# Weight halves of the pair products interleaved word by word in their ring tiles

## The chip, the cores and the metric

The kernel runs on one core of a Trainium2 chip. The metric is the device time of one execution in microseconds (us); lower is better. Five engines work at the same time, each through its own queue in order: TensorE (PE; its weight loads are shown apart as PEld), VectorE (DVE), ScalarE (ACT), GpSimd (POOL) and SyncE (SP), which issues nearly all transfers.

## The reference: what is computed

Two requests of 512 tokens of width 1024 go through the same two layers, each of which adds the output of a mixer to its input:

```python
for i in range(DEPTH):                       # 2
    h = rms_norm(x, norm_g[i], NORM_EPS)
    if i % 2 == 0:
        x = x + diff_attention(h, ...)       # proj = h @ w_in -> q, k, v, gate; o @ w_out
    else:
        x = x + bidir_retention(h, ...)      # proj = h @ w_in -> q, k, v, gate; o @ w_out
return rms_norm(x, final_norm_g, NORM_EPS)
...
proj = h @ w_in                              # (512, 1024) @ (1024, 8192) in layer 0, 6144 columns in layer 1
q, k, v, gate = jnp.split(proj, [...], axis=-1)
```

All in float32. The change concerns the big input projections `h @ w_in` of both layers, for the columns that become q, k and gate.

## The kernel before

**Numbers in two halves.** A float32 operand is split in two: the upper half is the value as a copy into the type fp32r leaves it, the lower half is the rest (value minus upper half, again as fp32r). A product takes three matmuls (`PASSES`: upper x upper, upper x lower, lower x upper), summed in PSUM. The helper `hi_of` (line 399) writes the upper half by a copy on ScalarE (it shows as L400 CAST), `lo_of` (line 402) the lower one by a subtraction on VectorE that reads the upper half back (L403).

**Projection units.** The projections are cut into units (class `Unit`, line 518), each for 256 columns of one weight matrix at two column groups or blocks, computed for both requests. A unit is not done with eight block products but with seven (`SEQ`: P1, P2, P5, P6, P3, P7, P4), each of sums and differences of weight blocks with sums and differences of activation blocks, and the outputs are put together from the seven results. The activation side (`Bop`, made by `make_b`) is split once and lies in SBUF tiles of [128, 2, 512], upper half first, in the tiles named arena and b. The weight side is loaded in raw tiles, combined on VectorE (`combine`, L558, into st tiles) and split into ws tiles, a ring of `WS_BUFS = 7` places of 1024 words per partition.

There are two kinds of units:

- **pair** units (q, k and gate: 24 in the first layer, 16 in the second). The weights are the *stationary* operand: for each of four k-blocks a 128x128 piece of the ws tile is loaded into TensorE, and 512 columns of the activation side stream past. One product is 4 x 3 = 12 matmuls 128x512, each with its own weight load (`pair`, line 596; L599). Both halves of a 128-column block fit in one ws tile: `[P, 2, 4, n]` with n = 128, the upper half in the first 512 words, the lower half in the other 512.
- **wide** units (v). Here the activation side is stationary and the ws tile streams past 256 columns at a time (`wide`, line 603; L609). Each half takes a ws tile of its own.

For the rotary units (q and k) the raw columns are taken in another order: `half_view` (line 944) in the first layer takes runs of 64 columns, `parity_view` (line 947) in the second takes the even and then the odd columns, so that the engines read raw with a step of two words.

**Order.** `projections` (line 778) prepares the splits ahead of the products as far as the seven ws places allow. Every operation is entered in a `Plan` with an estimated cost for its engine; `Plan.arrange` (line 138) plays the engines through by these costs and writes out the order for each queue. The engines then run in that order and wait for each other by semaphores. The attention of the first layer (L1116, L1134, L1181) and the retention of the second (L1315 to L1367) come after the projections of their layer, with the output projections (L891) worked in between.

Of the kernel before, what the change touches and what calls it, by code (L numbers as in the profile page):

```python
# [15 lines left out]
P = 128  # L16
# [237 lines left out]
def trunk_kernel(  # L254
# [42 lines left out]
    def work(tag, shape, bufs, dt=F32, name=None):  # L297
        size = SIZE.get(tag, shape[1])
        return Buf(plan, tag, bufs, lambda i: view(wk, tag, i, size, shape, dt))
# [27 lines left out]
    def ws_t(shape):  # L327
        return work("ws", shape, WS_BUFS, F32R)
# [4 lines left out]
    def st_t(shape, name="st"):  # L333
        return work("st", shape, 3, name=name)
# [36 lines left out]
    def dve(n, fn, r, w, wait=0.0):  # L371
        plan.op("DVE", 0.07 + 0.00104 * n, fn, r, w, wait=wait)
# [26 lines left out]
    def hi_of(n, dst, src, r, w):  # L399
        act(n, lambda: nc.scalar.copy(dst(), src()), r, w)  # L400

    def lo_of(n, dst, src, hi, r, w):
        dve(n, lambda: nc.vector.tensor_tensor(dst(), src(), hi().bitcast(F32), op=ALU.subtract), r, w)  # L403
# [114 lines left out]
    class Unit:  # L518
# [32 lines left out]
        def prep(self, op):  # L551
            x = self.take
            n = 256 if self.wide else P

            def combine(a, b, fn):
                t = st_t([P, 4, n])
                out = ((lambda: self.like(t.t)), t)
                dve(4 * n, lambda: nc.vector.tensor_tensor(out[0](), a[0](), b[0](), op=fn), [a[1], b[1]], [t])  # L558
                return out
            if op == "P1":  # L560
                src = x(0, 0)
            elif op == "P2":
                src = x(0, 1)
            elif op == "P4":
                src = x(1, 1)
            elif op == "P5":
                src = self.s[1] = combine(x(1, 0), x(1, 1), ALU.add)
            elif op == "P6":
                src = self.s[2] = combine(self.s[1], x(0, 0), ALU.subtract)
            elif op == "P3":  # L570
                src = combine(x(0, 1), self.s[2], ALU.subtract)
            else:
                src = combine(x(0, 0), x(1, 0), ALU.subtract)
            if self.wide:
                a, b = ws_t([P, 4, n]), ws_t([P, 4, n])
                hi, lo = ((lambda: a.t), a), ((lambda: b.t), b)
            else:
                s = ws_t([P, 2, 4, n])
                hi, lo = ((lambda: s[:, 0]), (s, 0)), ((lambda: s[:, 1]), (s, 1))
            hi_of(4 * n, lambda: self.like(hi[0]()), src[0], [src[1]], [hi[1]])  # L580
            lo_of(4 * n, lambda: self.like(lo[0]()), src[0], lambda: self.like(hi[0]()), [src[1], hi[1]], [lo[1]])
            self.ops[op] = (hi, lo)
            if op == "P2" and self.early is not None:
                self.early, self.x = None, {}
# [949 lines left out]
```

## Time and profile before

| | |
|---|---|
| median of 3 runs | 1809.73 us (1808.83 to 1810.48) |
| span of the profiled execution, first to last instruction | 1807.0 us |
| median of the runs less that span | 2.7 us |
| granted TensorE clock, mean | 0.999 |
| TensorE busy | 1794.9 us (99%), 10299 matmuls |
| weight loads (PEld) busy | 1558.1 us (86%) |
| VectorE busy | 1477.1 us (82%) |
| ScalarE busy | 895.1 us (50%) |
| GpSimd busy | 169.5 us (9%) |

The profile lists the span of the profiled execution; that execution's time with what lies ahead of the first and behind the last instruction isn't listed apart, so the median of the runs stands in for it. In rows of groups the columns are: line, engine, operation, output<-inputs by the program's tile names, shapes, count, then busy time in us and mean ns of one, then idle time of the engine ahead of the group and what ended it. Busy time counts overlapping instructions once; the mean ns of one is its full length, overlap included. A line can be a helper's, so L400 and L403 stand for all splits of the kernel, told apart by their tiles.

### The profile page before, as it was taken

Reading aid. Unit: us, or ns where it says so; the run is one execution under the profiler, and the core shown is the slowest. Engines: PE = TensorE matmul, PEld = TensorE weight load, DVE = VectorE, ACT = ScalarE, POOL = GpSimd, SP = SyncE. Lnnn points to the kernel's source line nnn. Section 1 sums busy time; section 2 is a strip of 40 time slices with the busy share of each in tenths; the row PEclk is TensorE's granted clock in tenths of the full one; section 3 lists DMA queues with packets and bytes.
Section 4 is the critical chain, followed back from the end, with each engine's and each line's share of the span. In section 5 each row is a group of like instructions: output and inputs, shape, how many; then the busy total and the mean of one; then the engine's idle time right before and its main releaser. Section 6 shows DMA issues by size and latency. Waiting matters only on the chain.

```text
span 1807.0 us, 27780 instructions
## 1 busy us (share of the span) xinstructions
PE 1794.9 (99%) x10299; PEld 1558.1 (86%) x10299; DVE 1477.1 (82%) x2319; ACT 895.1 (50%) x1856; POOL 169.5 (9%) x323
## 2 busy tenths in 40 slices
PE   9999999999999999999999999999999999999998
PEld 6789889898988888888888888898989898888887
DVE  7958787778699888888888897787887967888887
ACT  7753444433434565554555866444434355444346
POOL 1000000000000022222322300000000000111113
PEclk9999999999999999999999999999999999999999
DMA  6444455555545685444554524464657559765662
GB/s 217 134 126 137 161 140 178 184 168 155 174 126 175 201 334 198 178 156 159 190 204 140 190 73 146 140 210 146 205 156 228 151 170 396 272 238 182 225 218 94
DMA packets 162767, 328.81 MB, mean 182 GB/s; under 512 B 12724, under 2 KB 76872, under 8 KB 162632
## 3 DMA queue, kind: packets, MB, share of 16 engines
q1 hardware_dynamic: 162304, 326.71, 54.1%
q8 instruction: 81, 1.33, 0.3%
q14 instruction: 54, 0.44, 0.1%
q10 hardware_dynamic: 328, 0.34, 0.1%
HBM read 209.55 MB, written 117.44 MB: 181 GB/s over the span
## 4 chain that ended last, share of the span: by engine, by line
PE 93%; DVE 2%; DMA 2%; ACT 2%; issue 1%; POOL 0%; SPq 0%; POOLq 0%; DVEq 0%; ACTq 0%
PE pj L599 20%; PE pj L891 19%; PE sc L599 10%; PE pj L609 10%; PE o L599 8%; PE o L1181 5%; PE sc L1116 5%; PE sc L609 5%; PE o L609 2%; PE o L1359 2%; PE tp L1161 2%; PE sc L1315 1%; PE o L1367 1%; PE tp L1339 1%; DMA raw<-in_ret_w_out_dram 1%
## 5 line engine op out<-in xcount | busy, mean ns | idle before, releaser
L891 PE MATMUL pj<-ws,arena 128*128 128x512 f32 x1542 | 391.2, 397 | 0.0
L891 PEld LDWEIGHTS pj<-ws,arena 128*128 128x128 f32 x1542 | 277.7, 188 | 52.7
L599 PE MATMUL pj<-b,ws 128*128 128x512 f32 x1080 | 265.0, 392 | 0.0
L599 PEld LDWEIGHTS pj<-b,ws 128*128 128x128 f32 x1080 | 201.4, 188 | 43.0
L403 DVE TENSOR_TENSOR ws<-st,ws 128x512 fp32r<-128x512 f32 (+1 forms) x192 | 147.9, 774 | 74.8 <-ACT ws L400 56.7
L896 DVE SCALAR_TENSOR_TENSOR b<-pj,crr,b 128x512 f32<-128x512 f32 (+1 forms) x257 | 189.9, 744 | 21.4 <-PE pj L891 21.0
L403 DVE TENSOR_TENSOR ws<-raw,ws 128x512 fp32r<-128x512 f32 (+1 forms) x164 | 141.5, 868 | 71.3 <-ACT ws L400 61.0
L400 ACT CAST ws<-st 128x512 fp32r<-128x512 f32 (+1 forms) x192 | 132.4, 693 | 121.4 <-PE pj L599 36.4
L599 PE MATMUL sc<-arena,ws 128*128 128x512 f32 x768 | 186.8, 392 | 0.0
L599 PE MATMUL o<-arena,ws 128*128 128x512 f32 x744 | 180.0, 393 | 1.1 <-ACT m L385 0.6
L599 PEld LDWEIGHTS sc<-arena,ws 128*128 128x128 f32 x768 | 144.0, 188 | 31.3
L400 ACT CAST ws<-raw 128x512 fp32r<-128x512 f32 (+1 forms) x164 | 125.7, 772 | 87.0 <-PE o L599 45.0
L599 PEld LDWEIGHTS o<-arena,ws 128*128 128x128 f32 x744 | 138.4, 188 | 31.7 <-DVE arena L463 1.4
L599 PE MATMUL pj<-arena,ws 128*128 128x512 f32 x648 | 160.3, 392 | 0.4 <-DVE arena L463 0.4
L599 PEld LDWEIGHTS pj<-arena,ws 128*128 128x128 f32 x648 | 120.8, 188 | 26.7 <-DVE arena L463 0.7
L1134 ACT ACTIVATE b<-sc,nm 128x512 f32<-128x512 f32 x128 | 88.0, 689 | 66.9 <-DVE nm L1124 66.5
L636 ACT COPY c<-pj 128x512 f32<-128x512 f32 x104 | 60.9, 586 | 119.7 <-PE pj L599 66.4
L609 PE MATMUL pj<-ws,b 128*128 128x256 f32 x960 | 116.8, 276 | 0.0
L609 PEld LDWEIGHTS pj<-ws,b 128*128 128x128 f32 x960 | 113.2, 188 | 0.7
L1116 PE MATMUL sc<-arena 128*128 128x512 f32 x384 | 101.2, 395 | 0.3 <-ACT b L1134 0.3
L1181 PEld LDWEIGHTS o<-arena 128*128 128x128 f32 x768 | 93.1, 188 | 2.7
L1181 PE MATMUL o<-arena 128*128 128x256 f32 x768 | 93.7, 278 | 0.0
(207 smaller groups left out, 2855.9 us busy)
## 6 DMA issues: line engine op xcount, KB each, us to landing
qk<-os SPq DMA_DIRECT2D x192, 256.0 KB, 3.6
arena<-qk SPq DMA_DIRECT2D x96, 512.0 KB, 5.8
raw<-in_da_w_in_dram SPq DMA_DIRECT2D x64, 512.0 KB, 5.1
v<-os SPq DMA_DIRECT2D x64, 512.0 KB, 4.3
arena<-v SPq DMA_DIRECT2D x64, 512.0 KB, 4.1
raw<-in_ret_w_in_dram SPq DMA_DIRECT2D x48, 512.0 KB, 4.8
os<-g SPq DMA_DIRECT2D x32, 512.0 KB, 7.4
g<-e SPq DMA_DIRECT2D x48, 256.0 KB, 4.6
```

The costliest lines, as they stand in the source:

```text
L400: act(n, lambda: nc.scalar.copy(dst(), src()), r, w)
L403: dve(n, lambda: nc.vector.tensor_tensor(dst(), src(), hi().bitcast(F32), op=ALU.subtract), r, w)
L599: nc.tensor.matmul(ps.t, a[u][0]()[:, k, :], bt[k][:, v, :], start=(opens and k == 0 and i == 0), stop=(k == 3 and i == 2), skip_group_che ...
L609: nc.tensor.matmul(ps[:, (t % 2) * 256:(t % 2) * 256 + 256], bt[k][:, v, t * P:(t + 1) * P], a[u][0]()[:, k, :], start=(opens and t % 2 == ...
L636: act(S, lambda c=c, ps=ps: nc.scalar.copy(c.t, ps.t), [ps], [c])
L891: nc.tensor.matmul(ps[:, here], o[a][:, e, t * P:(t + 1) * P], u[b][:, e, here], start=(m == 0), stop=(m == 5))
L896: axpy(n, lambda half=half, here=here, ps=ps: nc.vector.scalar_tensor_tensor(half, ps[:, here], rr[:, t % 2:t % 2 + 1], half, op0=ALU.mult ...
L1116: nc.tensor.matmul(s.t, q[:, a, t * P:(t + 1) * P], k[:, b, :], start=(n == 0), stop=(n == 2))
L1134: act(840, lambda j=j, s=s, m=m: nc.scalar.activation(p[:, j, :], s.t, AF.Exp, bias=m.t, accum_out=sm[:, 2 * j + n:2 * j + n + 1]), [s, m] ...
L1161: nc.tensor.transpose(tp[:, j * P:(j + 1) * P], p[:, 0, j * P:(j + 1) * P], ident.t)
L1181: nc.tensor.matmul(o[:, e * 256:(e + 1) * 256], v[b][:, j, e * P:(e + 1) * P], aT[a][:, j, :], start=(n == 0), stop=(n % 12 == 11), skip_g ...
L1359: nc.tensor.matmul(o[:, e * 256:(e + 1) * 256], v_[v][:, 2 * c + j, e * P:(e + 1) * P], a_[:, u, j * 256:(j + 1) * 256], start=(e == 0 and ...
```

## The change

The ws tile of a pair unit keeps its size and its place. Its two halves no longer lie one behind the other: upper and lower half of each weight stand next to each other. So the ScalarE copy writes every second word, the VectorE subtraction reads every second word and writes the words between, and each 128x128 weight load of a pair product reads 128 words with a step of two words.

```diff
             else:
-                s = ws_t([P, 2, 4, n])
-                hi, lo = ((lambda: s[:, 0]), (s, 0)), ((lambda: s[:, 1]), (s, 1))
+                s = ws_t([P, 4, n, 2])
+                hi, lo = ((lambda: s[:, :, :, 0]), (s, 0)), ((lambda: s[:, :, :, 1]), (s, 1))
             hi_of(4 * n, lambda: self.like(hi[0]()), src[0], [src[1]], [hi[1]])
             lo_of(4 * n, lambda: self.like(lo[0]()), src[0], lambda: self.like(hi[0]()), [src[1], hi[1]], [lo[1]])
```

## The prediction

> **What bounds the kernel now.** I read the page first, then the groups by line with shapes kept apart, the waits of PE, the chain of waits in order of time, the timeline around one product, and last the busy time of the engines in stretches of 100 us.
>
> ```profile
> span 1807.0 us, 27780 instructions
> ...
> PE 1794.9 (99%) x10299; PEld 1558.1 (86%) x10299; DVE 1477.1 (82%) x2319; ACT 895.1 (50%) x1856; POOL 169.5 (9%) x323
> ...
> PE 93%; DVE 2%; DMA 2%; ACT 2%; issue 1%; POOL 0%; SPq 0%; POOLq 0%; DVEq 0%; ACTq 0%
> ```
>
> TensorE is busy for 99% of the span and holds 93% of the chain that ended last. A busy TensorE need not be one at its best rate, so the question is what sets the distance from one matmul to the next, and whether TensorE ever waits for the tiles that the change touches.
>
> ```profile
> L599 PE MATMUL pj<-b,ws 128*128 128x512 f32 x1080 | 265.0, 392 | 0.0
> L599 PEld LDWEIGHTS pj<-b,ws 128*128 128x128 f32 x1080 | 201.4, 188 | 43.0
> L609 PE MATMUL pj<-ws,b 128*128 128x256 f32 x960 | 116.8, 276 | 0.0
> L609 PEld LDWEIGHTS pj<-ws,b 128*128 128x128 f32 x960 | 113.2, 188 | 0.7
> L599 PE MATMUL sc<-b,ws 128*128 128x512 f32 x120 | 29.1, 391 | 0.0
> ```
>
> Columns: busy time and mean ns of one, then idle time ahead of them. "pair" products are line 599, "wide" ones line 609. The pair matmuls stand in five groups: pj from b (1080), sc from arena (768), o from arena (744), pj from arena (648), sc from b (120); the first and the last are shown, the sum is 3360. That is 40 pair units of 7 products of 12 matmuls, each with a weight load of its own, and every one of these loads gets the step of two.
>
> ```profile
> PE sc L1010 <- DVE minus L411: 1.4, 1, 1.4
> ...
> PE tp L815 <- DVE b L403: 0.2, 1, 0.2
> ```
>
> Eight rows in all, 4.8 us together, and none names a ws tile: TensorE has not once waited for a split weight.
>
> ```profile
> 327.85 5.47 PE pj L609 x48
> 555.21 8.24 PE pj L599 x36
> ```
>
> The chain's pieces give the pitch: 8.24 us for 36 pair matmuls is 0.2289 us each; 5.47 us for 48 wide ones is 0.1140 us each. Half the columns, half the pitch (twice 0.1140 is 0.2280), although both load 128x128 weights for every matmul. So the pitch follows the columns that stream past, not the load: a load costs at most 0.114 us of the weight port, or two of the wide matmuls could not follow each other so closely. The 188 ns that a load is shown with is therefore not the time it holds anything: loads of 188 ns begin every 114 ns.
>
> ```profile
> 409.65 2.59 PEld L599 LDWEIGHTS o<-arena,ws 128*128 128x128 f32 x12
> 409.76 2.91 PE L599 MATMUL o<-arena,ws 128*128 128x512 f32 x12
> 412.51 0.39 PE L599 MATMUL sc<-arena,ws 128*128 128x512 f32 x1
> ```
>
> Here a wide product ends and a pair product begins: the first load of the pair product starts at 409.65, its matmul at 409.76, 0.11 us later; the next product's first matmul comes 2.75 us (12 times 0.229) after it. Load time some 0.11 us, pitch 0.229 us: a pair load may become 2.0 to 2.1 times as long before TensorE notices it.
>
> **The change, edit by edit.** The order of the instructions on all five engines is the same before and after, and so are their counts and TensorE's waits. Sixteen VectorE splits and one ScalarE copy lose a wait for TensorE; as TensorE is the bound and VectorE is ahead of it, that is worth nothing. No DMA is touched. What changes is the step, in three places.
>
> ```profile
> L403 DVE TENSOR_TENSOR ws<-st,ws 128x512 fp32r<-128x512 f32 x160 | 108.9, 685 | 56.7 <-ACT ws L400 56.2
> L400 ACT CAST ws<-st 128x512 fp32r<-128x512 f32 x160 | 98.7, 621 | 74.9 <-PE pj L599 30.3 <-issue 13.1 <-PE sc L599 11.1
> L403 DVE TENSOR_TENSOR ws<-raw,ws 128x512 fp32r<-128x512 f32 x108 | 73.1, 685 | 24.3 <-ACT ws L400 18.2 <-PE pj L609 5.6
> L403 DVE TENSOR_TENSOR ws<-raw,ws 128x1024 fp32r<-128x1024 f32 x56 | 68.4, 1221 | 47.0 <-ACT ws L400 42.8 <-PE pj L891 3.0 <-ACT os L400 1.1
> L400 ACT CAST ws<-raw 128x1024 fp32r<-128x1024 f32 x56 | 58.8, 1049 | 9.8 <-DMA raw<-in_ret_w_out_dram 8.0 <-DMA raw<-in_da_w_out_dram 1.8
> L403 DVE TENSOR_TENSOR ws<-b,ws 128x512 fp32r<-128x512 f32 x12 | 7.9, 680 | 0.0
> ```
>
> *The split's two writes.* 280 pair splits (160 from st, 108 from raw, 12 from b) each have a ScalarE copy (621 ns) that writes the upper half and a VectorE subtract (685 ns) that reads that half and writes the lower. Writes of step two occur nowhere in this trace. Their bounds: nothing, if the step is free; and the price of passing over all 1024 places of the tile, the two 1024-element rows: 1221 - 685 = 0.536 us more on VectorE, 1049 - 621 = 0.428 us more on ScalarE. A gain there would move nothing, because neither engine holds TensorE. For reads the trace does have a step of two: in the second layer the rotary units take even and odd columns (parity_view, line 948), and between 1217 and 1425 us all pair splits from raw are of this kind.
>
> ```profile
> L403 DVE TENSOR_TENSOR ws<-st,ws 128x512 fp32r<-128x512 f32 x24 | 16.3, 688 | 10.7 <-ACT ws L400 10.7
> L403 DVE TENSOR_TENSOR ws<-raw,ws 128x512 fp32r<-128x512 f32 x17 | 11.5, 686 | 3.8 <-ACT ws L400 3.8
> L400 ACT CAST ws<-raw 128x512 fp32r<-128x512 f32 x17 | 11.0, 661 | 19.7 <-PE o L599 16.2 <-PE pj L609 2.6 <-PE pj L599 0.9
> L400 ACT CAST ws<-st 128x512 fp32r<-128x512 f32 x24 | 14.7, 621 | 12.0 <-PE pj L599 6.4 <-issue 2.9 <-PE sc L599 2.8
> L558 DVE TENSOR_TENSOR st<-raw,raw 128x512 f32<-128x512 f32 x5 | 3.4, 684 | 0.0
> ```
>
> VectorE: 686 ns with one source at step two against 688 without, and 684 with both sources so (st from raw, raw). Free. ScalarE: 661 against 621, so 0.04 us more. The writes go over the same spread of addresses as these reads, which makes them the nearest rows: I take nothing for VectorE, whose read of the upper half is free by the same rows, and 0.04 us for ScalarE, 280 x 0.04 = 11 us of its time in the whole span.
>
> ```profile
> core 0: us, PE busy (x) PEld busy (x) DVE busy (x) ACT busy (x) POOL busy (x), PEclk, DMA share, GB/s
> 500.00:600.00 100.00, 100.00 (x439) 82.04 (x438) 93.96 (x152) 40.12 (x71) 0.00 (x0) 1.00 0.48 143
> 1000.00:1100.00 100.00, 99.17 (x493) 82.18 (x492) 91.24 (x147) 74.53 (x163) 11.72 (x16) 1.00 0.45 150
> ```
>
> These are the two stretches where pair splits are many and VectorE is fullest. ScalarE has 60 and 25 us to spare in them, VectorE 6.0 and 8.8.
>
> ```profile
> L403 DVE TENSOR_TENSOR ws<-st,ws 128x512 fp32r<-128x512 f32 x21 | 14.4, 685 | 1.3 <-ACT ws L400 0.8
> L403 DVE TENSOR_TENSOR ws<-raw,ws 128x512 fp32r<-128x512 f32 x15 | 10.3, 687 | 2.0 <-ACT ws L400 1.5
> ```
>
> ```profile
> L403 DVE TENSOR_TENSOR ws<-st,ws 128x512 fp32r<-128x512 f32 x16 | 10.9, 681 | 2.3 <-ACT ws L400 2.3
> L403 DVE TENSOR_TENSOR ws<-raw,ws 128x512 fp32r<-128x512 f32 x7 | 4.7, 682 | 0.0
> L403 DVE TENSOR_TENSOR ws<-b,ws 128x512 fp32r<-128x512 f32 x6 | 4.0, 684 | 0.0
> ```
>
> 36 splits in the first stretch, 29 in the second. 36 x 0.04 = 1.4 us on ScalarE disappears in its 60. A later upper half makes the lower one later by the same 0.04 us; what covers this is the ring of seven ws tiles, which lets splits run up to six pair products of 2.75 us ahead. Were that cover gone, the cost would be 280 x 0.04 = 11 us. VectorE would have to grow by 6.04 / 36 = 0.17 us a split before the first stretch is full.
>
> The Trainium skill speaks against the change here. "Vector Engine (DVE) Microarchitecture Reference", section 5.2 (Measured stream behaviour on trn2), says that a port runs at full rate only where its elements come in runs of at least two adjacent 4-byte words, and gives 1.71 ns per column instead of 1.054 for a destination that hops at each element; by that a split would take an estimated 0.34 us longer. The rows above do not show it for reads at a step of two. "SBUF - State Buffer" (section "Door 1: The DMA port swizzle") has another rule, 16-byte lines that want two hits each, and a step of two in fp32 gives just two; VectorE's rows agree with it, ScalarE's 0.04 us only nearly.
>
> *The load.* 3360 loads read 128 words out of 256 places instead of 128. No load with a step is in the trace. Below: no gain, since the load sets no pitch today. Above: if the load passes over all 256 places it takes twice 0.110 to 0.114, 0.220 to 0.228 us, and still ends inside the 0.2289. Another comparison: the moving operand takes 512 words in 0.2289 us, 2.2 words per ns over addresses; a step-two load at today's speed passes 256 word places in 0.11 us, 2.3 per ns, the rate that a port of TensorE already runs at. I take a load up to a tenth longer, as on ScalarE, hidden: 0.
>
> Sum: 0 (loads) + 0 (VectorE) + 0 on the path (ScalarE's 11 us hidden) against the span of 1807.0. The median of the runs, 1809.73, lies 2.7 us over that span; this remains. **Forecast 1809.7 us, no change** (a measurement here can tell about 0.2%, 3.6 us).
>
> **Rivals.**
>
> *The load becomes the bound (slower).* Place: all 3360 pair matmuls. It decides from the point where a step-two load takes more than 0.229 us. Price: if each of the 128 words needs a fetch of its own, and a fetch takes as long as the moving stream needs for four words (0.2289 / 128 = 1.79 ns), the fetches alone are 0.229 us; what of today's 0.11 us is not fetching comes on top, between nothing and 0.11 - 32 x 1.79 ns = 0.053 us. So 0 to 3360 x 0.053 = 178 us; in the middle 89, giving 1899. For it: a load with a step was never seen here. Against it: the two comparisons above. 17%.
>
> *Loads and moving reads get in each other's way (slower).* With the step both ports pass through addresses at nearly the same rate, so if they meet they keep meeting. That the pitch can vary while width and loads stay the same is shown by two pieces of one line:
>
> ```profile
> 768.19 2.73 PE o L1181 x24
> 950.58 2.83 PE o L1181 x24
> ```
>
> 24 matmuls in 2.73 or in 2.83 us: 4 ns each. On 3360 matmuls 1 to 5 ns are 3.4 to 17 us; at 4 ns 13.4, giving 1823. Against it: pair products keep 0.229 whichever ring tile and operand they use. 15%.
>
> *VectorE becomes the bound (slower).* If the write costs 0.536 us more, the first stretch holds 93.96 + 36 x 0.536 = 113.3 us of work, the second 91.24 + 29 x 0.536 = 106.8: 20 us too much, giving 1830. It decides from 0.17 us per split. Against it: the free reads. 12%. By the skill's 1.71 ns the same sum would be 6.2 + 1.1 us over, an estimated 1817.
>
> *Faster.* Only a shorter pitch could do it, and the nearest row for one is twice the wide pitch: 0.9 ns less, 3.0 us in all, giving 1806.7. For more than that no row speaks. 7%.
>
> That the step doesn't reach the load is no case: the operand of the matmul is the strided half itself.
>
> **How the numbers follow.** No change 49%, load-bound 17%, ports in each other's way 15%, VectorE 12%, faster 7%. Predicted 1809.7. The range goes down to 1805, past the 1806.7, and up to 1845: it takes in the cases of 1823 and 1830 with their bounds, and the load-bound case up to 0.010 us a matmul (34 us). Left out are most of the load-bound case, some 13%, and half of the gain. The likeliest case's own range is 1807 to 1813. Faster by over 0.2%: 0.07; within: 0.49; slower: 0.17 + 0.15 + 0.12 = 0.44.
>
> **What would show it.** Right: pieces of 36 pair matmuls still 8.24 us in the chain, VectorE's ws from st at 685 ns, ScalarE's copies into pair tiles near 660 ns, no ws row among PE's waits. Load-bound: the same pieces longer than 8.3 us and equal everywhere, wide ones unchanged at 5.47. Ports: pitch up by a few ns, differing by tile. VectorE: 0.85 us and more for its writes, new PE waits for ws or for banks that VectorE empties around 500 to 600 and 1000 to 1100 us. The forecast is wrong if the time leaves 1806 to 1813.

## The result, and the profile after

The changed kernel takes 1832.89 us (median of 4 runs, 1832.72 to 1833.08), the kernel before 1809.61 beside it: a ratio of 1.0129, 95% interval 1.0115 to 1.0142. That is 23.3 us more, 1.3%. Single executions of the kernel before spread further than its medians do: of the 50 beside all the runs here five took 1814.0 to 1815.1 us, and as none of these was traced, what made them longer is not known.

The page of the kernel after, its span, its busy times and the head of its chain, then three of its costliest groups (busy time and mean ns of one, then idle time ahead of them):

```profile
span 1830.9 us, 27771 instructions
...
PE 1818.6 (99%) x10299; PEld 1591.6 (87%) x10299; DVE 1478.3 (81%) x2319; ACT 904.6 (49%) x1856; POOL 171.6 (9%) x323
...
PE 94%; DVE 2%; ACT 2%; issue 1%; DMA 1%; POOL 0%; SPq 0%; POOLq 0%; ACTq 0%
...
L599 PE MATMUL pj<-b,ws 128*128 128x512 f32 x1080 | 269.4, 396 | 0.0
L599 PEld LDWEIGHTS pj<-b,ws 128*128 128x128 f32 x1080 | 209.1, 195 | 40.0
...
L609 PE MATMUL pj<-ws,b 128*128 128x256 f32 x960 | 120.9, 281 | 0.0
```

The span grew by 23.9 us and TensorE's busy time by 23.7. VectorE has 1.2 us more and ScalarE 9.5, and their shares of the chain stay at 2%. The strided loads are shown with 195 ns instead of 188, seven more. The odd row is the third group's: line 609, the wide products, was not touched, and went from 116.8 to 120.9 us.

The splits, from the groups of the kernel after with shapes kept apart:

```profile
L403 DVE TENSOR_TENSOR ws<-st,ws 128x512 fp32r<-128x512 f32 x160 | 109.1, 686 | 60.6 <-ACT ws L400 60.6
L400 ACT CAST ws<-st 128x512 fp32r<-128x512 f32 x160 | 104.9, 661 | 83.4 <-PE pj L599 31.8 <-issue 13.2 <-PE sc L599 11.5
```

VectorE's strided write costs 1 ns, ScalarE's 40 ns (661 against 621).

Where TensorE's time went is read from the chain of waits around the first wide unit (start in us, length in us, engine, tile, line, count). First the kernel before, then the kernel after, whose last line here is a piece of 36 pair matmuls from elsewhere in the span:

```profile
160.83 2.75 PE pj L599 x12
163.58 5.47 PE o L609 x48
169.04 5.44 PE sc L609 x48
...
190.81 2.75 PE pj L599 x12
193.55 5.47 PE pj L609 x48
```

```profile
157.17 0.44 PE pj L606 x4
157.61 5.46 PE pj L609 x48
163.07 2.80 PE pj L599 x12
165.87 5.65 PE o L609 x48
171.53 5.65 PE sc L609 x48
...
194.14 2.79 PE pj L599 x12
196.93 5.65 PE pj L609 x48
...
508.84 8.40 PE pj L599 x36
```

A pair matmul went from 8.24 / 36 = 0.2289 to 8.40 / 36 = 0.2333 us, 4.4 ns more, and 3360 of them make 14.9 us. A wide matmul behind the pair product at 163.07 went from 5.44 / 48 = 0.1133 to 5.65 / 48 = 0.1177 us, the same 4.4 ns. Per wide unit that is 0.18 + 4 x 0.21 + 0.18 = 1.2 us (the first and the last of these six pieces were at 5.47), and eight units make 9.6 us. Together 24.5, an estimate from one place of each kind, where the span grew by 23.9. But this wide unit's first product, at 157.61, is still at 5.46, though strided pair products run right up to 157.17; between them stand only four transposes. (In the next three wide units no transposes stand there, and the first product is slow too, 5.65 or 5.66.) So the same instructions have two rates, and a product has the one or the other; I call them the quick rhythm (0.1133 wide, 0.2289 pair) and the slow one (0.1177, 0.2333).

### The profile page after: what moved, and what is told of

Its sections match the earlier page's. It is cut to its first block, busy times and chain, and to the rows that moved or that the text cites. A ratio compares the mean times of both kernels' runs of the same rounds, so it can differ in the third digit from the quotient of the medians.

```text
span 1830.9 us, 27771 instructions
## 1 busy us (share of the span) xinstructions
PE 1818.6 (99%) x10299; PEld 1591.6 (87%) x10299; DVE 1478.3 (81%) x2319; ACT 904.6 (49%) x1856; POOL 171.6 (9%) x323
## 4 chain that ended last, share of the span: by engine, by line
PE 94%; DVE 2%; ACT 2%; issue 1%; DMA 1%; POOL 0%; SPq 0%; POOLq 0%; ACTq 0%
PE pj L599 21%; PE pj L891 18%; PE sc L599 11%; PE pj L609 10%; PE o L599 8%; PE sc L609 5%; PE o L1181 5%; PE sc L1116 5%; PE o L609 2%; PE o L1359 2%; PE tp L1161 2%; PE sc L1315 1%; PE o L1367 1%; PE tp L1339 1%; DVE ws L403 1%
## 5 line engine op out<-in xcount | busy, mean ns | idle before, releaser
L599 PE MATMUL pj<-b,ws 128*128 128x512 f32 x1080 | 269.4, 396 | 0.0
L599 PEld LDWEIGHTS pj<-b,ws 128*128 128x128 f32 x1080 | 209.1, 195 | 40.0
L400 ACT CAST ws<-st 128x512 fp32r<-128x512 f32 (+1 forms) x192 | 138.6, 726 | 134.8 <-PE pj L599 38.9
L400 ACT CAST ws<-raw 128x512 fp32r<-128x512 f32 (+1 forms) x164 | 129.4, 795 | 94.6 <-PE o L599 42.8
L599 PEld LDWEIGHTS sc<-arena,ws 128*128 128x128 f32 x768 | 149.5, 195 | 29.2
L599 PEld LDWEIGHTS o<-arena,ws 128*128 128x128 f32 x744 | 143.6, 195 | 29.6 <-DVE arena L463 1.3
L599 PEld LDWEIGHTS pj<-arena,ws 128*128 128x128 f32 x648 | 125.4, 195 | 24.9 <-DVE arena L463 0.6
L609 PE MATMUL pj<-ws,b 128*128 128x256 f32 x960 | 120.9, 281 | 0.0
L609 PEld LDWEIGHTS pj<-ws,b 128*128 128x128 f32 x960 | 117.1, 189 | 0.6
```

The source lines that it names most:

```text
L599: nc.tensor.matmul(ps.t, a[u][0]()[:, k, :], bt[k][:, v, :], start=(opens and k == 0 and i == 0), stop=(k == 3 and i == 2), skip_group_che ...
L609: nc.tensor.matmul(ps[:, (t % 2) * 256:(t % 2) * 256 + 256], bt[k][:, v, t * P:(t + 1) * P], a[u][0]()[:, k, :], start=(opens and t % 2 == ...
```

## The experiments

**Which half of the change.** The first kernel keeps the strided writes and loads contiguously; it reads wrong words.

```
         s = ws_t([P, 4, n, 2])                       # as in the changed kernel
-        ps.t, a[u][0]()[:, k, :], bt[k][:, v, :], ...
+        ps.t, loaded(self, a[u], k, u), bt[k][:, v, :], ...
+def loaded(unit, q, k, u):
+    s = q[1][0].t.rearrange("p a b c -> p (a b c)")
+    return s.rearrange("p (u k n) -> p u k n", u=2, k=4)[:, u, k, :]
```

> Both halves are stored interleaved as in the changed kernel, but each weight load of a pair product reads 128 words in a row (so wrong words of the right tile: the output isn't the reference's). Load theory (the step of the load costs TensorE 4.4 ns per pair matmul and leaves the weight path in a state that costs wide matmuls about as much): 1809 to 1811 us, 36 pair matmuls 8.24 us, 48 wide ones 5.47 us, ScalarE's copies still 661 ns. Store theory (the spaced stores of ScalarE and VectorE get in the way of all TensorE reads of the projections): 1833 us, 8.40 and 5.65 us.

1809.81 us, ratio 1.0003 (0.9994 to 1.0013). A piece of its chain:

```profile
133.08 8.24 PE pj L599 x36
```

The second keeps the contiguous writes and steps the loads by two, over the same addresses of the same tiles as the changed kernel; it reads wrong words.

```
+def loaded(unit, q, k, u):
+    s = q[1][0].t.rearrange("p a b c -> p (a b c)")
+    return s.rearrange("p (k n two) -> p k n two", k=4, two=2)[:, k, :, u]
```

> Both halves are stored one behind the other as before, but each weight load of a pair product reads 128 words with a step of two over the same addresses as in the changed kernel (wrong words, the output isn't the reference's). Load theory: 1833 us, 36 pair matmuls 8.40 us, 48 wide ones 5.65 us, ScalarE's copies 621 ns. Store theory: 1809 to 1811 us, 8.24 and 5.47 us.

1833.37 us, ratio 1.0132 (1.0116 to 1.0147), with loads shown at 195 ns and pieces of 8.40 and 5.65 us, as in the changed kernel. The writes cost nothing that these runs can tell; the step of the load is the whole loss.

**How the price goes with the step.** The halves are stored as before, and the loads have a step of four, then of three (wrong words again):

```
+    s = q[1][0].t.rearrange("p a b c -> p (a b c)")[:, k * 128 + u:k * 128 + u + 128 * STEP]
+    return s.rearrange("p (n w) -> p n w", w=STEP)[:, :, 0]
```

> Stores as before, each weight load of a pair product reads 128 words with a step of four (wrong words, the output isn't the reference's). Load theory, if the load's time goes by the addresses it spans: the load doubles again to some 0.21 to 0.23 us, pair pitch 0.235 to 0.245 us, 1830 to 1870 us; if any step that is not one costs the same: 1833 us with a pitch of 0.2333 us. Store theory: 1809 to 1811 us.

> Loads step three everywhere (3360), data laid out as before; it reads wrong words. If the load grows with the span that it reads beyond 1024 bytes (195 ns at step two, 312 at step four): about 250 ns shown, and its pair pitch lies between 233.3 and 240.0 ns, 8.4 to 8.65 us for 36. If the slow state of the wide products goes with step two alone, they are at 5.47 and the total is 1809.6 + 3360 x (4.4 to 11 ns) = 1824 to 1847 us, middle 1836; if it goes with any load below some length, step three has it too and the total is 1836 to 1857.

Step four: 1846.24 us, ratio 1.0202 (1.0187 to 1.0218). Step three: 1830.58, ratio 1.0116 (1.0101 to 1.0132), less than step two costs. Loads, a piece of pair products and a wide product behind a strided pair product, for step four and then for step three:

```profile
L599 PEld LDWEIGHTS pj<-b,ws 128*128 128x128 f32 x1080 | 265.9, 312 | 0.1
...
76.64 8.64 PE pj L599 x36
...
169.21 5.45 PE o L609 x48
```

```profile
L599 PEld LDWEIGHTS pj<-b,ws 128*128 128x128 f32 x1080 | 254.8, 252 | 0.1
...
76.35 8.48 PE pj L599 x36
...
167.10 5.45 PE o L609 x48
```

The shown load goes 188, 195, 252, 312 ns for steps one to four, the pair pitch 228.9, 233.3, 235.6, 240.0. But behind the pair products the wide ones are quick again at steps three and four, nearly everywhere. So the slow rhythm behind the pair units is not what a longer load brings by itself. Step three's total, below step two's, comes from there. The exceptions show that these steps can meet the slow rhythm too. At step four the wide product at 160.59, behind four transposes, takes 5.66 us. At step three six pair products of the second layer run at 0.2333 us a matmul and not at 0.2356 (the twelve from 1175.03 take 2.80 us), and behind four of them twelve wide matmuls stand 117.9 ns apart. The load is shown at 252 to 253 ns in either place. So one stepped load goes with two pitches, and 0.2356 is not set by the load's length alone.

**How long it lasts.** Step two only in the eight pair units that stand right ahead of a wide unit, 672 loads of 3360 (wrong words in these):

```
+def mark(units):
+    for u, after in zip(units, units[1:]):
+        u.spaced = after.wide and not u.wide       # the others load contiguously
```

> Stores as before; the step of two only in the loads of the eight pair units that stand right before a wide unit (672 of 3360 loads; wrong words there, the output isn't the reference's). The last product of such a unit runs between the first and the second product of the wide unit. Load theory with a state that lasts: the wide products stay at 5.65 us per 48 although none of their operands has a step, 672 x 4.4 ns + 2688 x up to 4.2 ns = 3 to 14 us more, about 1822 us. Load theory without such a state: wide products at 5.47 us, 3 us more, 1813 us. Store theory: 1809 to 1811 us.

1822.24 us, ratio 1.0069 (1.0052 to 1.0086). The price by load would be 672 x 4.4 ns = 3.0 us; it is 12.9. The chain shows unstrided work that pays the rest:

```profile
187.64 5.65 PE pj L609 x48
193.29 2.77 PE pj L599 x12
196.06 5.65 PE pj L609 x48
201.71 2.76 PE o L599 x12
```

None of the loads in these rows has a step. The wide product at 196.06 is still slow, and the stream goes back, by way of 2.76, in the pair products behind it. It does not stay slow all the way: in the pair product of 2.77 the last seven matmuls stand 228.6 ns apart, the quick pitch, and the wide product behind them is slow again. In the other seven wide units the pair product there takes 2.80 us and the wide one behind it 5.46, quick.

Then step two in one product of each of those units only, its last (P4, between the wide unit's first product and its second): 12 loads, 96 in all.

```
-            a, b = self.ops.pop(op), B_OF[op]
+            a, b = self.ops.pop(op), B_OF[op]; last = self.next and op == "P4"   # self.next: a wide unit follows
```

> Loads step by two in one product only of each pair unit ahead of a wide unit: its last (P4, the one that stands between the wide unit's first product P1 and its second); 12 loads there, 96 of 3360 in all. It reads wrong words in them. If a slow state is entered by a single strided product and lasts over the unstrided matmuls behind it: the wide products behind P4 show 5.65 us for 48 (P1 stays at 5.47), 8 units x about 288 matmuls x 4.3 ns = 9.9 us, together about 1819.5 us (1816 to 1821). If each strided load costs only its own matmul, or the state needs a whole unit of them: 96 x 4.4 ns = 0.4 us, 1810.0 us (1809 to 1811.5), wide products at 5.47.

1818.83 us, ratio 1.0052 (1.0037 to 1.0067): 9.2 us for 96 loads. Its chain:

```profile
156.42 5.46 PE pj L609 x48
161.88 2.80 PE pj L599 x12
164.69 5.65 PE o L609 x48
...
187.30 5.66 PE pj L609 x48
192.95 2.80 PE pj L599 x12
195.75 5.46 PE pj L609 x48
201.22 2.75 PE o L599 x12
```

Only the twelve loads at 161.88 have a step. The 240 wide matmuls behind them are slow, and so is the pair product at 192.95, whose loads are contiguous: 2.80 us, just what a strided one takes. Behind it the stream is quick. So a pair matmul's 4.4 ns need no step of its own; they belong to the rhythm.

**Fewer strided loads.** Step two in the lower half's loads alone, every third load (`if not (u == 1): return q[0]()[:, k, :]`), then in one load of the twelve of each pair product, the last (`k == 3 and u == 1`) or the third (`k == 0 and u == 1`). All three read wrong words in these loads.

> Only the loads of the lower half step by two: every third load, 1120 of 3360; the upper ones are contiguous; it reads wrong words. If each strided load lengthens its own matmul by 4.4 ns and the state comes from a run of them: 1120 x 4.4 = 4.9 us, 1814.5 us (1813 to 1816), wide pieces 5.47. If a few strided loads hold TensorE's weight loads in the slow state, contiguous ones between them too: all pair pieces 8.40 and wide ones 5.65, 1833 us (1829 to 1834).

> Of the twelve loads of each pair product only the last (k = 3, the lower half) steps by two: 280 of 3360; it reads wrong words in them. If a single strided load puts TensorE into the slow state and the next unstrided matmuls stay in it: wide pieces 5.65 us, 8 units x 240 x 4.4 ns = 8.4 us, and pair matmuls at 233.3 for 14.8 us more, or for a part of that if contiguous pair loads leave the state within a product: 1818 to 1833 us. If the price is by load: 280 x 4.4 = 1.2 us, 1810.8 us (1809.5 to 1812), wide pieces 5.47.

> As the run with the last load strided, but it is the third of the twelve (k = 0, the lower half), so that nine contiguous pair loads follow before any wide product. If those nine end the state: wide pieces 5.47, pair products slow for a part of their twelve, 1810 to 1817 us. If the state lasts over contiguous pair loads too: as the other run within 2 us, wide pieces 5.65. By load: 1810.8 us.

Every third: 1826.90 us, 1.0097 (1.0080 to 1.0114), pair pieces of 8.32 us, wide ones 5.65; neither figure expected, between the two. Last of twelve: 1824.58, 1.0084 (1.0069 to 1.0099). Third of twelve: 1825.59, 1.0089 (1.0072 to 1.0106). So 280 loads cost 15 to 16 us, 54 to 58 ns each, where all 3360 cost 24.0 us, 7 ns each. The nine contiguous loads after the third do not end it: its wide units are slow in seven of eight cases. With the last load strided it was five of eight; two of its wide products, of the first and the third unit:

```profile
165.42 5.65 PE o L609 x48
...
380.82 5.45 PE o L609 x48
```

Behind the same strided load the rhythm came out slow in one place and quick in the other.

**A break in the stream.** If it is a rhythm, restarting the stream should change it. In the changed kernel, four transposes against the identity ahead of each wide unit's second product; that product's first matmul overwrites what they write:

```
-                if self.led and op == "P1" and t == 0:
+                if t == 0 and (op == "P2" or self.led and op == "P1"):
                     for j in range(NT):
                         nc.tensor.transpose(ps[:, j * P:(j + 1) * P], ident.t, ident.t)
```

> The changed kernel, with four transposes against the identity (each 0.109 us, with no strided load) put ahead of every wide unit's second product, behind the strided P4; the products' first matmul overwrites what they write. They cost 8 x about 0.45 us = 3.6 us. If any short stretch of other work on TensorE ends the slow state: wide pieces go back to 5.47 us from there up to the next strided pair product, about 8 x 192 to 288 matmuls x 4.3 ns = 6.6 to 9.9 us less, together 1826 to 1830 us. If the state needs more than that to end, or comes from how the wide products' operands lie in this kernel: pieces stay at 5.65, 1836 to 1837.5 us.

1833.00 us, ratio to the kernel before 1.0131 (1.0115 to 1.0146), no better than the changed kernel without them. Its chain, in the first wide unit and the fifth:

```profile
163.29 2.80 PE pj L599 x12
166.09 0.44 PE o L606 x4
166.53 5.46 PE o L609 x48
...
193.74 2.80 PE pj L599 x12
196.55 5.66 PE pj L609 x48
...
1193.46 5.66 PE o L609 x48
```

In four wide units of eight the break ends the slow rhythm until the next strided product; in the other four it doesn't. Four units win 0.19 + 4 x 0.21 = 1.0 us each, and the transposes themselves take 8 x 0.44 = 3.5 us. The total lies between the two that were expected. The same break in the kernel before, where no load has a step:

> The kernel before with the same four transposes ahead of each wide unit's second product as in the run on the changed kernel: the price of the breaks alone. 8 x (4 x 0.109 + about 0.09 for the restart) = 4.2 us, so 1813 to 1814 us; if the breaks end the slow stretches behind pair products in this kernel too (48 matmuls at 115.5 and 113.9 ns against 113.3) it is up to 1 us less. If the price turns out at 10 us or more, the changed kernel with the breaks (1833.0) had saved what the ended state should bring, and the breaks ate it.

1821.46 us, ratio 1.0065 (1.0050 to 1.0080), 12 us where the transposes account for 3.5:

```profile
164.03 0.44 PE o L606 x4
164.47 5.65 PE o L609 x48
...
192.74 2.80 PE pj L599 x12
195.54 5.46 PE pj L609 x48
```

Without any step in the kernel the same slow rhythm stands behind the break, over the same 240 matmuls and one pair product, in all eight units. 8 x 240 x 4.4 ns = 8.4 us, and 3.5 for the transposes, make 11.9. So the rhythm is not the step's own; a step is one way into it. Left open was whether transposes as a kind of work bring it, or the moment at which the stream goes on behind them. Three and one in place of four, in the kernel before:

```
-                    for j in range(NT):
+                    for j in range(3 if op == "P2" else NT):     # and 1 in the other kernel
```

> The kernel before with three transposes instead of four ahead of each wide unit's second product. If transposes as a kind of work bring the slow rhythm: wide pieces behind them 5.65 us, about 1821 us (1820 to 1822.5). If it hangs on when the stream starts again: three may land it in the other rhythm, pieces of 5.44 to 5.47 us in all or some units, about 1813 us (1812 to 1818).

> As that, with one transpose. By kind of work: 5.65 us pieces, about 1820 us (1818.5 to 1821.5). By the time of the restart: 5.44 to 5.47 us in all or some units, 1810.5 to 1817 us. If three and one give the same rhythm as four in every unit, the place in time is not shown to matter.

Three: 1811.36 us beside 1808.61, ratio 1.0015 (1.0001 to 1.0028). One: 1811.53, ratio 1.0011 (1.0002 to 1.0020). A chain piece of the first, then two places of the second:

```profile
163.27 0.33 PE o L606 x3
163.60 5.46 PE o L609 x48
```

```profile
163.22 5.46 PE o L609 x48
...
297.62 5.66 PE o L609 x48
```

Three transposes leave the quick rhythm in all eight units and cost their own 8 x 0.33 = 2.6 us. Four leave the slow one in all eight. One leaves the quick one in six and the slow one in two, 8 x 0.11 + 2 x 1.1 = 3.1 us. One transpose at eight like places leads into both rhythms, so the kind of work does not decide.

Nor do the instructions by themselves. Up to the first break TensorE runs the same ones, in the same order, in the kernel before and in the three made from it. Among them are four transposes that every kernel has ahead of its first wide unit. The wide product behind those, in the kernel before and in the one with breaks of four:

```profile
155.37 5.46 PE pj L609 x48
```

```profile
155.60 5.66 PE pj L609 x48
```

With breaks of three it takes 5.66 us, with breaks of one 5.46. The changed kernel shows the same: 5.46 without the breaks, 5.66 with them, ahead of the first break. So one and the same sequence came out in either rhythm. Each kernel was traced in one execution, so the counts of units are those of that execution; the medians (1821.46 against 1811.36) say that four and three differ in most others too. What does differ is the moment at which the wide stream goes on: by 0.11 us from kernel to kernel, by some ns from place to place. That it decides was not shown. From the start of the last pair matmul to that of the first wide one the kernel with one transpose has 259 ns ahead of three quick products and ahead of a slow one too.

## Why the prediction was wrong, point by point

**The forecast and the range.** No change was forecast, with 1807 to 1813 as that case's own range, and it did not come: 1832.89. That this lies inside the stated 1805 to 1845 is luck, since the range was stretched for rivals of other kinds. The nearest of their times, VectorE's 1830, is luck as well: VectorE was busy for 1.2 us more, and its place in the chain did not grow.

**The bound** was right: the loss is TensorE's own. Its waits after, nine rows with 5.1 us in all, name no ws tile; the last of them:

```profile
PE tp L1040 <- ACT b L385: 0.2, 1, 0.2
```

**The splits' writes** were right: 686 ns on VectorE against 685 and 661 on ScalarE against 621, the very rows of the strided reads, and with contiguous loads the kernel takes 1.0003 of its time before. So the VectorE rival has no case. The rule of the Trainium skill that spoke for it ("Vector Engine (DVE) Microarchitecture Reference", section 5.2: full rate only for runs of at least two adjacent 4-byte words) is not borne out by these writes. The 1.71 ns a column that it gives, and that the prediction took over, is for a destination hopping 4 KiB at each element; a step of two words is not among its rows.

**The load, hidden: 0** is the step that failed. The sum put the loads at nothing, and the runs showed the whole 23.3 us there, by the estimates above 14.9 in the pair matmuls and 9.6 in the wide ones. The prediction read from the quoted pieces that "the pitch follows the columns that stream past, not the load", and so that a pair load may become 2.0 to 2.1 times as long before TensorE notices. The shown load became 7 ns longer, and the pitch 4.4 ns. Nor does the margin hold further out: at step three the load is shown 64 ns longer, 0.110 + 0.064 = 0.174 us by the prediction's count and still well inside 0.229, and the pitch is 0.2356. Having room beside the moving stream is not the same as costing it nothing. The row that it read had a hint of it: the wide products of 5.47 us are those right behind a pair product, and the ones that follow take 5.44. In the trace the 0.03 us is four or five matmuls at 117 ns and more, before the pitch falls to 113.3. And the term counted only the matmuls whose loads change; 1.2 us per wide unit fell on loads that do not.

**The rival "the load becomes the bound"** asked for pair pieces over 8.3 us, equal everywhere, and wide ones unchanged. The pieces are 8.40, nearly equal everywhere, but the load is far from 0.229: it priced up to 0.053 us a matmul, and step two adds 0.0044, step four 0.0111.

**The rival "loads and moving reads get in each other's way"** came closest in kind: at its 4 ns it gave 1823, and the 4.4 ns of the pair products alone would give 1824.6. It expected them to differ by tile, and they do not; it left out the wide products, which give the other 9.6 us by the estimate above. Its evidence, the two pieces of line 1181 with 24 matmuls in 2.73 and 2.83 us, is 113.8 and 117.9 ns: by their size the two rhythms, in the kernel before. The prediction took them for reads that meet in one tile and not in another. Whether line 1181 is slow there for the same reason was not tried.

**What is shown, and what is open.** Shown: the step of the load is the whole loss; the unstrided matmuls pay a part of it; the slow rhythm outlasts its cause, over 240 wide matmuls and on to a pair product with contiguous loads; and with no step at all, a short break puts the stream into it, or does not, even where the instructions ahead are the same. Not shown: what inside TensorE's load and read paths holds the two rhythms, what decides between them behind a break, why step two leaves the slow one behind nearly everywhere and steps three and four in few places, and what sets the pair pitch at those steps (235.6 and 240.0). A meeting of weight reads and moving reads would fit all of it, but it was only argued. No kernel here beats the one before.

## What to carry to other kernels

Weights that load beside a moving stream are not free because they fit beside it: try the access pattern on the real stream and read the distance between matmuls, not the length of the load. When a change touches one kind of matmul, compare the pitch of the others too; a cost can stand in instructions that nobody edited. And before pricing a small change that adds or shifts work on TensorE, look in the trace for two rates of the same instruction: one transpose more, 0.1 us at eight places, moved 8.4 us of matmuls here.

## What was not expected of the hardware

Back-to-back matmuls, each with its own contiguous 128x128 load, have two steady rates that differ by 4.4 ns per matmul, for 256 columns (113.3 and 117.7 ns) and for 512 (228.9 and 233.3) alike, at a granted clock of 0.999 in both kernels. Each held over 240 wide matmuls, 28 us. In the kernel before, four transposes of 0.44 us together led into the slow one eight times of eight, three of 0.33 us never, one of 0.11 us twice; in the changed kernel four ended it four times of eight (one execution of each kernel). Behind the same instructions both rates occurred: 5.46 and 5.66 us for the same 48 matmuls. A step-two load is shown at 195 ns, step three at 252, step four at 312, against 188 contiguous.
